# Mixer stage reordered: state-space tiles projected before pool tiles, block copies as transfers, trailing sums on GpSimd

## The chip, the cores and the metric

The kernel runs on one core of a Trainium2 chip. The metric is device time in microseconds (us) from start to end of one execution. The core has five engines that work side by side, each through its own instructions in order: TensorE (PE in the profile, with its weight loads as PEld), VectorE (DVE), ScalarE (ACT), GpSimd (POOL) and SyncE (SP), whose queue here issues nearly all DMAs. They wait for each other on semaphores.

## What is computed

One layer of a decoder for 256 prompt rows and 8 sample rows, model width D = 2048, all weights in float32:

```python
# per layer, c conditions shift, scale and gate (adaLN)
x += 1/2 * g1 * SwiGLU_1(mod1(RMSNorm(x)))              # FFN width 5632
[u ; v] = mod2(RMSNorm(x)) @ W_in                       # u: S5 half, v: pooling half, 1024 each
x += g2 * ([GLU(GELU(Re(C s) + D u)) ; scale * Lin_g(mean_w(v) - v)] @ W_out)
x += 1/2 * g3 * SwiGLU_2(mod3(RMSNorm(x)))
y = RMSNorm(x)
```

s is the state of a diagonal complex recurrence, s_t = A s_(t-1) + B u_t, with 64 groups of 16 channels and 64 states. mean_w is a trailing mean over w = 2, 4, 8, 16 rows, for four groups of 256 channels. The states and the last 15 pooling rows are outputs too.

## The kernel before

**Tiling.** Activations lie with channels on partitions: 16 blocks (kt) of 128 channels by N = 264 columns. A big product is a sum over 16 blocks of k, each in three passes of TensorE (hi·xh, hi·xl, lo·xh, L404 to L406 in `mm3`). The weights come as raw tiles of 512 KB, eight 128x128 blocks each, on SP's queue (L153, five buffers); ScalarE makes the high part hi (L190), VectorE the rest lo (L192). Among them run the "ada" steps: the modulation vectors of later sublayers, eight matmul rows each with two raw tiles of their own (L310), and once in 16 steps a transpose (adaT, L314) and a sum (mod) on VectorE.

**Stages.** FFN1 in groups, the mixer, FFN2, the last norm. The mixer is W_in, the two halves, and W_out. W_in has 16 output tiles. They came in the order 8 to 15 (pooling) and then 0 to 7 (S5). The first FBI = 5 are computed together in `first_block`, k by k, while the normalised input arrives, and the others one by one (48 matmuls each).

**A pool tile** (`pool_tile`): two ScalarE copies out of PSUM, then trailing sums by doubling, w = 16 taking four steps of shifted adds (sA, sB) and w = 2 one; then five small operations make z. All adds ran on VectorE. `pool_lin` multiplies a group's z by its 256x256 matrix pw.

**An S5 tile** ft has four steps. `s5_v`: u is copied out of PSUM (L976), and 16 block copies (L982, half on VectorE and half on ScalarE) lay u out as V, shifted by 64 columns for each of four rows of 32 partitions; two ScalarE operations make bx. `s5_e`: 8 matmuls make E from V and bx (L998), 4 begin y's PSUM tile from V (L1002), 8 add the sample state (L1005). Then a chain of VectorE operations, each on the one before: as, za and zb from E, two scans (L1016), and S in its real and imaginary half. GpSimd meanwhile makes ca from Cm in twelve operations; ca has one buffer. `s5_y`: 32 matmul rows add ca·S to y's PSUM tile (L1050), and GELU follows on ScalarE and VectorE. `s5_g`: one matmul with gluw (L1063), tanh, and the insert into `mixed` on VectorE. `conv` splits `mixed` into Xh and Xl for W_out.

**What sets the order.** The program's text gives the priority, a scheduler of the framework sets one order of instructions for each engine, and the engine then keeps to it: a waiting instruction holds everything behind it. In the text E(ft−1) stands in W_in tile ft after k block 9, y(ft−2) after that tile. The last E, y and g of the S5 tiles stood inside W_out, by `wout_plan`.

Of the kernel before, what the change touches and what calls it, by code (L numbers as in the profile page):

```python
# [50 lines left out]
W_OUT_K = list(range(8, 16)) + list(range(0, 8))  # L51
# [44 lines left out]
def win_order():  # L96
    o = []
    ms = list(range(8, 16)) + list(range(0, 8))
    for kt in range(KT):
        o += [("i", kt, m) for m in ms[:FBI]]  # L100
    for m in ms[FBI:]:
        o += [("i", kt, m) for kt in range(KT)]
    return o


def wout_plan():
    pool, ssm = W_OUT_K[:8], W_OUT_K[8:]
# [9 lines left out]
    mm((2, 3), pool)  # L117
    p += [("g", 6)]
    mm((0, 1, 2, 3), ssm[0:4])
    p += [("y", 7)]  # L120
    mm((0, 1, 2, 3), ssm[4:7])
    p += [("g", 7)]
    mm((4,), pool)
    mm((0, 1, 2, 3), ssm[7:8])
    mm((4,), ssm)
    for m in range(5, KT):
        mm((m,), W_OUT_K)
    return p
# [81 lines left out]
def build(nc, tc, I, O):  # L210
# [459 lines left out]
    def first_block(pool, gh, gl, rb, n):  # L670
# [8 lines left out]
        for i, ps in enumerate(pss):  # L679
            g = pool.tile([P, N], F32, tag=f"fb{i}", name=f"fb{cnt[0]}_{i}", bufs=1)  # L680
# [199 lines left out]
    with tc.tile_pool(name="mix", bufs=1) as mp:  # L880
        mixed = mp.tile([P, KT, N], F32, tag="mixed", name="mixed")
        with tc.tile_pool(name="poolp", bufs=1) as qp:
            rb, samples, one = make_h(qp, mods[3], mods[4], GP)
            pw = qp.tile([P, 4, 2, 256], F32, tag="pw", name="pw")
# [6 lines left out]
            vsm = qp.tile([P, 8, NS], F32, tag="vsm", name="vsm")  # L891

            def pool_tile(mt, ps, z):
# [15 lines left out]
                if w >= 8:  # L909
                    add(sA[:, :, 2:66], sB[:, :, 2:66], sB[:, :, 1:65])  # L910
                    s = sA
                if w >= 16:
                    add(sB[:, :, 2:66], sA[:, :, 2:66], sA[:, :, 0:64])
                    s = sB
# [5 lines left out]
                add(zz[:, SEQ:N], vsm[:, mt, :], hsum[:, mt, :])  # L920
                stt(zz[:, SEQ:N], zz[:, SEQ:N], 1.0 / w, vsm[:, mt, :], ALU.mult, ALU.subtract)

            def pool_lin(g, z):
                for m2 in range(2):
                    ps = bank()
                    for k2 in range(2):
                        T.matmul(ps[:, 0:N], lhsT=pw[:, g, k2, m2 * P:(m2 + 1) * P], rhs=z[:, k2, :], start=(k2 == 0), stop=(k2 == 1))
# [5 lines left out]
            def new_z(g):  # L933
                zs[g] = qp.tile([P, 2, N], F32, tag="z", name=f"z{g}", bufs=3)

            pss = first_block(qp, X1[0], X1[1], rb, FBI)
            for a in range(0, KT, SG):
                for kt in range(a, a + SG):
                    one(kt)
                samples(a, a + SG)  # L940
            tc.keep_in_program_order(nc.sync.dma_start(out=pw, in_=I["poolw"]))

            def u_tile(hook=None):
                ps = bank()
                for kt in range(KT):
                    mm3(ps[:, 0:N], st.get(), Xh[:, kt, 0:N], Xl[:, kt, 0:N], kt == 0, kt == KT - 1)
                    if hook is not None:
                        hook(kt)
                return ps

            for mt in range(FBI):
                if mt % 2 == 0:
                    new_z(mt // 2)
                pool_tile(mt, pss[mt], zs[mt // 2])
            lin = {6: 1, 7: 2, 5: 0}
            for mt in range(FBI, 8):
                ps = u_tile()
                if mt in lin:
                    pool_lin(lin[mt], zs[lin[mt]])
                if mt % 2 == 0:  # L960
                    new_z(mt // 2)
                pool_tile(mt, ps, zs[mt // 2])
            ps = u_tile()
            pool_lin(3, zs[3])
            A.dma_start(out=O["vout"], in_=vout)
            A.dma_start(out=O["vsm"], in_=vsm)

        with tc.tile_pool(name="s5p", bufs=1) as sp:
            Vb = [sp.tile([P, 4, N], F32, tag=f"V{i}", name=f"V{i}") for i in range(2)]
            for t in Vb:  # L970
                GP.memset(t, 0.0)
            S5 = {}

            def s5_v(ft, ps):
# [16 lines left out]
            def s5_e(ft):  # L991
# [17 lines left out]
                a = sp.tile([P, 2, 4, C], F32, tag="za", name=f"za{ft}", bufs=1)  # L1009
                b = sp.tile([P, 4, C], F32, tag="zb", name=f"zb{ft}", bufs=1)  # L1010
# [7 lines left out]
                S = sp.tile([P, 2, 4, C + 1], F32, tag="S", name=f"S{ft}", bufs=2)  # L1018
# [7 lines left out]
                ca = sp.tile([P, 2, 4, 4, 32], F32, tag="ca", name=f"ca{ft}", bufs=1)  # L1026
                cb = sp.tile([P, 4, 2, 32], F32, tag="cb", name=f"cb{ft}", bufs=1)
# [16 lines left out]
            def s5_y(ft):  # L1044
# [6 lines left out]
                y2 = sp.tile([P, N], F32, tag="y2", name=f"y2{ft}", bufs=1)  # L1051
                gy = sp.tile([P, N], F32, tag="gy", name=f"gy{ft}", bufs=1)
# [7 lines left out]
            def s5_g(ft):  # L1060
# [3 lines left out]
                t = sp.tile([P, N], F32, tag="y2", name=f"gt{ft}", bufs=1)  # L1064
# [3 lines left out]
            s5_v(0, ps)  # L1068
# [11 lines left out]
            conved = set()  # L1080

            def conv(kt):
                if kt in conved:
                    return
                conved.add(kt)
                if kt < NFT:
                    A.activation(out=Xh[:, kt, 0:N], in_=mixed[:, kt, :], func=AF.Copy, scale=0.25)
                    stt(Xl[:, kt, 0:N], mixed[:, kt, :], 0.25, Xh[:, kt, 0:N].bitcast(F32), ALU.mult, ALU.subtract)
                else:
                    A.copy(out=Xh[:, kt, 0:N], in_=mixed[:, kt, :])  # L1090
                    sub(Xl[:, kt, 0:N], mixed[:, kt, :], Xh[:, kt, 0:N].bitcast(F32))

# [13 lines left out]
            while plan:  # L1106
# [3 lines left out]
                else:  # L1110
                    {"g": s5_g, "e": s5_e, "y": s5_y}[a[0]](a[1])
                    if a == ("g", 7):
                        break
# [158 lines left out]
```

## Time and profile before

| | us |
|---|---|
| median of three runs (2086.51 to 2089.89) | 2087.66 |
| span of the profiled execution | 2090.6 |
| TensorE busy | 2033.3 (97%) |
| VectorE busy | 1212.7 (58%) |
| ScalarE busy | 842.3 (40%) |
| GpSimd busy | 410.6 (20%) |

No other time of the profiled execution is known than its span. It is within the runs' spread to 0.1%. In the mixer, the first W_in block begins near 954 us from the span's start, the second group at 997, the first E at 1041, the last y ends at 1186, and W_out ends at 1271. To read the rows: a row of the windows view has, for one stretch, each engine's busy time with its count of instructions, then the granted TensorE clock as a share of 2.4 GHz, the busy share of the DMA engines and their rate. A row of the timeline has the start, the duration, the engine, the line, the operation, output<-inputs, the shape and, in brackets, idle time before it and what ended it. Busy time of matmuls is longer at the lower clock, so a stretch can be busy and still lose time.

### The profile page before, as it was taken

The page shows a single profiled execution, that of the slowest core. Times are in us where ns is not written, and L with a number is a line of the kernel's source. Part 1 is how long each engine was busy: PE and PEld are TensorE (multiplying, and loading weights), DVE is VectorE, ACT ScalarE, POOL GpSimd, SP SyncE. Part 2 cuts the span into 40 slices and gives each one's busy share as a digit, 9 for nine tenths or more (in the row PEclk, how much of TensorE's full clock was granted, in tenths as well). Part 3 has the DMA queues.
Part 4 walks back from the last instruction along what each step waited for, and adds up shares of the span by engine and source line. Part 5 has one row for each costly group of instructions (what it writes and reads, how often), then busy time and mean ns, then how long its engine had stood idle before and what let it go on. Part 6 is the DMA issues. An engine that isn't in the chain of part 4 may idle for free.

```text
span 2090.6 us, 41113 instructions
## 1 busy us (share of the span) xinstructions
PE 2033.3 (97%) x16856; PEld 1870.3 (89%) x16856; DVE 1212.7 (58%) x1978; ACT 842.3 (40%) x1258; POOL 410.6 (20%) x713
## 2 busy tenths in 40 slices
PE   6999999999999999999988899999999999999997
PEld 5788999899999989998766698899999999999997
DVE  4665855754444454467789776545555555554555
ACT  4332434433333333355445355433334333334343
POOL 0000100330764068043345332000000000000012
PEclk9999999999999999999989999999999999999998
DMA  8888777777676776777844656875555555555552
GB/s 321 314 296 286 246 261 252 286 267 250 229 247 231 258 252 234 267 261 251 314 151 178 219 205 219 283 273 182 180 175 180 182 187 175 182 182 175 179 181 103
DMA packets 135292, 476.43 MB, mean 228 GB/s; under 512 B 15160, under 2 KB 20152, under 8 KB 134840
## 3 DMA queue, kind: packets, MB, share of 16 engines
q1 hardware_dynamic: 134384, 473.07, 64.6%
q8 instruction: 132, 2.16, 0.4%
q10 hardware_dynamic: 720, 0.75, 0.1%
q14 instruction: 56, 0.46, 0.1%
HBM read 471.20 MB, written 3.01 MB: 227 GB/s over the span
## 4 chain that ended last, share of the span: by engine, by line
PE 71%; issue 11%; POOL 8%; DVE 7%; DMA 2%; ACT 1%; SPq 0%; POOLq 0%; ACTq 0%; DVEq 0%
PE mm L404 22%; PE mm L406 21%; PE mm L405 21%; PE ada_None L310 3%; POOL xu L215 2%; DVE lo L192 2%; PE ada L328 2%; POOL yt L215 1%; DVE V L982 1%; POOL X L215 1%; DMA raw<-ada 1%; POOL acc L215 1%; POOL h L215 1%; DVE S L215 1%; PE E L998 1%
## 5 line engine op out<-in xcount | busy, mean ns | idle before, releaser
L192 DVE TENSOR_TENSOR lo<-raw,hi 128x1024 fp32r<-128x1024 f32 x591 | 733.5, 1241 | 610.4 <-ACT hi L190 584.5
L190 ACT CAST hi<-raw 128x1024 fp32r<-128x1024 f32 x592 | 619.7, 1047 | 1000.6 <-PE mm L405 777.9
L404 PE MATMUL mm<-Xh,hi 128*128 128x264 f32 (+1 forms) x3168 | 922.8, 292 | 2.4 <-ACT Xh L735 1.7
L405 PE MATMUL mm<-Xl,hi 128*128 128x264 f32 (+1 forms) x3168 | 910.6, 288 | 0.0
L406 PE MATMUL mm<-Xh,lo 128*128 128x264 f32 (+1 forms) x3168 | 906.6, 287 | 1.7 <-DVE lo L192 1.5
L404 PEld LDWEIGHTS mm<-Xh,hi 128*128 128x128 f32 x3168 | 600.6, 190 | 77.3 <-issue 59.8
L406 PEld LDWEIGHTS mm<-Xh,lo 128*128 128x128 f32 x3168 | 602.8, 191 | 8.8 <-issue 5.6
L405 PEld LDWEIGHTS mm<-Xl,hi 128*128 128x128 f32 x3168 | 602.5, 190 | 7.9 <-issue 7.6
L404 PE MATMUL mm<-ah,hi 128*128 128x264 f32 x1408 | 404.3, 287 | 0.0
L406 PE MATMUL mm<-ah,lo 128*128 128x264 f32 x1408 | 400.7, 285 | 0.0
L405 PE MATMUL mm<-al,hi 128*128 128x264 f32 x1408 | 398.8, 283 | 0.0
L404 PEld LDWEIGHTS mm<-ah,hi 128*128 128x128 f32 x1408 | 264.9, 188 | 21.0 <-issue 15.9
L405 PEld LDWEIGHTS mm<-al,hi 128*128 128x128 f32 x1408 | 265.3, 188 | 0.0
L406 PEld LDWEIGHTS mm<-ah,lo 128*128 128x128 f32 x1408 | 264.7, 188 | 0.0
L215 POOL TENSOR_TENSOR acc<-acc,sq 128x264 f32<-128x264 f32 x42 | 45.8, 1089 | 748.5 <-ACT sq L655 748.5
L310 PE MATMUL ada_None<-raw,sc 128*32 128x512 f32 x896 | 129.0, 608 | 8.2 <-DVE adaT_None L314 5.0
L232 DVE SCALAR_TENSOR_TENSOR x<-mm,mod,x 128x256 f32<-128x256 f32 x78 | 37.6, 482 | 42.1 <-PE mm L406 42.1
L215 DVE TENSOR_TENSOR s<-s,mm 128x264 f32<-128x264 f32 x68 | 29.1, 428 | 55.7 <-PE mm L406 55.7
L328 PE MATMUL ada<-raw,sc 128*32 128x256 f32 (+1 forms) x640 | 43.8, 374 | 14.0 <-DMA raw<-ada 13.9
L215 POOL TENSOR_TENSOR xu<-X,apow 128x128 f32<-128x128 f32 x96 | 53.6, 579 | 3.8
L215 POOL TENSOR_TENSOR s<-s,partBuT 128x264 f32<-128x264 f32 x7 | 5.3, 755 | 219.4 <-DVE partBuT L215 203.0
L310 PEld LDWEIGHTS ada_None<-raw,sc 128*32 128x32 f32 x896 | 19.3, 108 | 29.8 <-DMA raw<-ada 9.3
(303 smaller groups left out, 1471.6 us busy)
## 6 DMA issues: line engine op xcount, KB each, us to landing
raw<-w SPq DMA_DIRECT2D x528, 512.0 KB, 3.8
raw<-ada SPq DMA_DIRECT2D x288, 512.0 KB, 5.2
raw<-win SPq DMA_DIRECT2D x32, 512.0 KB, 5.1
raw<-wout SPq DMA_DIRECT2D x32, 512.0 KB, 4.3
x<-x SPq DMA_DIRECT2D x4, 528.0 KB, 5.7
xin<-x SPq DMA_DIRECT2D x16, 132.0 KB, 3.7
y<-o SPq DMA_DIRECT2D x7, 264.0 KB, 2.7
Cm<-Cm SPq DMA_DIRECT2D x1, 1024.0 KB, 5.8
```

Source lines behind the costliest of these rows:

```text
L190: c = self.nc.scalar.copy(out=hi, in_=raw)
L192: e.tensor_tensor(out=lo, in0=raw, in1=hi.bitcast(F32), op=ALU.subtract)
L215: return e.tensor_tensor(out=out, in0=a, in1=b, op=op)
L232: return e.scalar_tensor_tensor(out=out, in0=a, scalar=s, in1=b, op0=op0, op1=op1)
L310: T.matmul(ps[32 * j:32 * j + 32, :], lhsT=sc[:, kt, :], rhs=raws[j // 2][:, (j % 2) * 512:(j % 2 + 1) * 512], start=(kt == 0), stop=(kt = ...
L328: mm = T.matmul(o, lhsT=sc[:, kt, :], rhs=r[:, t, :, j, :], start=(kt == 0), stop=(kt == KT - 1))
L404: T.matmul(ps, lhsT=hi, rhs=xh, start=start, stop=False)
L405: T.matmul(ps, lhsT=hi, rhs=xl, start=False, stop=False)
L406: T.matmul(ps, lhsT=lo, rhs=xh, start=False, stop=stop)
L982: e(out=v[32 * tau:32 * tau + 32, q, 64 * tau:64 * tau + n], in_=u[32 * q:32 * q + 32, 0:n])
L998: T.matmul(E[:, ri, q * 72:(q + 1) * 72], lhsT=bx[:, ri, q].rearrange("p a b -> p (a b)"), rhs=v[:, q, 192:N], start=True, stop=True)
```

## The change

W_in's tiles come in the order 0 to 7 (S5), then 14, 15, 12, 13, 10, 11, 8, 9 (pool, widest window first). u goes straight into the places of `mixed` that pool tiles take later, and the 16 block copies of a tile are 16 DMAs from SBUF to SBUF on SP's queue, of 8 to 33 KB. The shifted adds and the sample sum run on GpSimd. In the text E(i) stands after k block 9 of the i-th single tile and y(i−1) behind that tile, so that all E, y and g lie inside W_in and none inside W_out; `pool_lin` of the groups 3, 2, 1 lie among the pool tiles, that of group 0 in W_out after 14 k blocks. pw comes in four loads rather than one. z has two buffers, not three. One pool ("heads") holds what two held in turn. FFN1 and the rest of the program keep their order.

```diff
-W_OUT_K = list(range(8, 16)) + list(range(0, 8))
+V_M = [14, 15, 12, 13, 10, 11, 8, 9]
+W_IN_M = list(range(8)) + V_M
+W_OUT_K = list(range(8)) + V_M
...
 def wout_plan():
...
-    mm((0, 1), pool[0:4])
-    p += [("g", 5), ("e", 7)]
-    mm((0, 1), pool[4:8])
-    p += [("y", 6)]
...
+    mm((0, 1), W_OUT_K[:14])
+    p.append(("l", 0))
+    mm((0, 1), W_OUT_K[14:])
+    for m in range(2, KT):
         mm((m,), W_OUT_K)
...
                 def sh2(o, s, d):
-                    add(o[:, d:4, 2:66], s[:, d:4, 2:66], s[:, 0:4 - d, 2:66])
-                    add(o[:, 0:d, 2:66], s[:, 0:d, 2:66], s[:, 4 - d:4, 1:65])
+                    add(o[:, d:4, 2:66], s[:, d:4, 2:66], s[:, 0:4 - d, 2:66], GP)
+                    add(o[:, 0:d, 2:66], s[:, 0:d, 2:66], s[:, 4 - d:4, 1:65], GP)
...
-                zs[g] = qp.tile([P, 2, N], F32, tag="z", name=f"z{g}", bufs=3)
...
+                pw = qp.tile([P, 2, 256], F32, tag="pw", name=f"pw{g}", bufs=2)
+                tc.keep_in_program_order(nc.sync.dma_start(out=pw, in_=I["poolw"][:, g]))
+                zs[g] = qp.tile([P, 2, N], F32, tag="z", name=f"z{g}", bufs=2), pw
...
-                u = sp.tile([P, N], F32, tag="u", name=f"u{ft}", bufs=1)
-                A.copy(out=u, in_=ps[:, 0:N])
+            def s5_v(ft):
+                u = mixed[:, V_M[ft], :]
                 v = Vb[ft % 2]
                 for q in range(4):
                     for tau in range(4):
                         n = N if tau == 0 else SEQ - 64 * tau
-                        e = (V.tensor_copy, A.copy)[(q + tau) % 2]
-                        e(out=v[32 * tau:32 * tau + 32, q, 64 * tau:64 * tau + n], in_=u[32 * q:32 * q + 32, 0:n])
...
+                        nc.sync.dma_start(out=v[32 * tau:32 * tau + 32, q, 64 * tau:64 * tau + n], in_=u[32 * q:32 * q + 32, 0:n])
...
-            for ft in range(1, NFT):
-                def hook(kt):
-                    if kt == 14 and ft >= 3:
-                        s5_g(ft - 3)
-                    if kt == 9:
-                        s5_e(ft - 1)
-                ps = u_tile(hook)
-                s5_v(ft, ps)
-                if ft >= 2:
-                    s5_y(ft - 2)
...
+            s5_v(0)
+            lin = {5: 3, 7: 2, 9: 1}
+            for i in range(KT - FBI):
+                ps = bank()
+                for kt in range(KT):
+                    mm3(ps[:, 0:N], st.get(), Xh[:, kt, 0:N], Xl[:, kt, 0:N], kt == 0, kt == KT - 1)
+                    if kt == 9 and i < NFT:
+                        s5_e(i)
+                    if kt == 14 and 2 <= i < NFT + 2:
+                        s5_g(i - 2)
...
+                if i + 1 < NFT:
+                    s5_v(i + 1)
+                if 1 <= i < NFT + 1:
+                    s5_y(i - 1)
+                if i in lin:
+                    pool_lin(lin[i])
```

**TensorE, E to y, before.** The third S5 tile's E, and y of the second behind it (a number in a name tells tiles apart; E_12475 is the third E, S_12307 comes from the second, E_12274).

```order
L998 MATMUL E_12475<-V_12038,bx_12366 128x72 x8
L1002 MATMUL mm_12484<-V_12038,KTp 32x264 x4
L1005 MATMUL mm_12484<-as_93,Cm 32x8 x8
L404 MATMUL mm_12411<-Xh,hi_12262 128x264
...
L1063 MATMUL mm_12546<-gy_12405,gluw 128x264
...
L1050 MATMUL mm_12283<-S_12307,ca_12316 32x64 x32
L310 MATMUL ada_None<-raw_12422,sc 32x512 x2
```

Left out are 14 W_in matmuls ahead of the gluw row and three behind it; y uses the S of the E before the one above.

**TensorE, E to y, after.** The third S5 tile from the middle of its E rows to the fourth tile's first E.

```order
L975 MATMUL E_12027<-V_11094,bx_11923 128x72 x5
L979 MATMUL mm_12036<-V_11094,KTp 32x264
L982 MATMUL mm_12036<-as_93,Cm 32x8 x8
L394 MATMUL mm_12168<-Xh,hi_12015 128x264
...
L300 MATMUL ada_None<-raw_11981,sc 32x512 x2
...
L1027 MATMUL mm_12036<-S_12060,ca_12069 32x64 x32
L300 MATMUL ada_None<-raw_12019,sc 32x512 x2
L975 MATMUL E_12219<-V_11095,bx_12123 128x72
```

S_12060 is made from E_12027, the E above it: between the Cm row and y stand 24 W_in matmuls and one ada step, and the next E stands one ada row behind y.

**VectorE, the chain in an S5 tile, before.** The second half of the second tile's chain (the row of L1016 is a scan).

```order
L215 TENSOR_TENSOR S_12307<-za_12297,Wr 128x4x64
L1016 SCALAR_TENSOR_TENSOR za_12297<-dec_12220,za_12297 128x256
L982 COPY V_12038<-u_12348 32x264
L215 TENSOR_TENSOR zb_12298<-za_12297,Wi 128x256
L215 TENSOR_TENSOR S_12307<-za_12297,Wr 128x4x64
L215 TENSOR_TENSOR S_12307<-S_12307,zb_12298 128x4x64
L982 COPY V_12038<-u_12348 32x128
L215 TENSOR_TENSOR zb_12298<-za_12297,Wi 128x256
```

**VectorE, the same place after**, in the fourth tile (z_12300 belongs to pool group 3, sB is a sum from GpSimd, sm a constant).

```order
L205 TENSOR_TENSOR S_12252<-S_12252,zb_12243 128x4x64
L222 SCALAR_TENSOR_TENSOR z_12300<-sB,vp_11085 128x256
L205 TENSOR_TENSOR zb_12243<-za_12242,Wi 128x256
L205 TENSOR_TENSOR z_12300<-sB,sm 128x4x4
L222 SCALAR_TENSOR_TENSOR z_12300<-z_12300,vsm 128x8
L205 TENSOR_TENSOR S_12252<-S_12252,zb_12243 128x4x64
```

The V copies are gone from the chain; in this tile z operations that need GpSimd's sB stand inside it.

On SP's queue, where raw tiles alone stood, the 16 transfers of a tile now stand in a row, with about five raw tiles between one tile's and the next; the four pw parts stand among them.

## Rows read from the trace of the kernel before

**Rows 1.** Page, part 1: busy time, share of the span, instructions of each engine.

```profile
PE 2033.3 (97%) x16856; PEld 1870.3 (89%) x16856; DVE 1212.7 (58%) x1978; ACT 842.3 (40%) x1258; POOL 410.6 (20%) x713
```

**Rows 2.** Windows: stretch, length, busy PE, PEld, DVE, ACT, POOL, clock, DMA share, GB/s.

```profile
953.00:1040.00 87.00, 85.46 (x609) 67.36 (x608) 67.74 (x176) 43.11 (x92) 26.85 (x49) 1.00 0.80 290
1050.00:1170.00 120.00, 100.69 (x1155) 82.49 (x1155) 110.88 (x208) 55.65 (x125) 63.71 (x103) 0.83 0.42 151
1170.00:1210.00 40.00, 37.34 (x330) 28.43 (x330) 25.61 (x44) 17.05 (x31) 11.55 (x18) 1.00 0.78 283
```

**Rows 3.** Waits of PE, 1050 to 1170: waiter <- releaser: us, times, longest.

```profile
PE E L998 <- DVE V L982: 10.6, 12, 1.6
PE ada_None L310 <- DVE adaT_None L314: 5.0, 1, 5.0
PE E L998 <- ACT gy L1053: 3.1, 2, 2.3
```

**Rows 4.** Windows of 10 us in the S5 stretch, columns as in rows 2.

```profile
1060.00:1070.00 10.00, 5.01 (x41) 3.34 (x33) 9.48 (x17) 5.02 (x13) 9.53 (x15) 0.90 0.30 107
1070.00:1080.00 10.00, 10.00 (x71) 8.26 (x64) 5.46 (x13) 1.33 (x2) 0.00 (x0) 0.58 0.60 211
...
1130.00:1140.00 10.00, 8.94 (x129) 6.86 (x127) 9.32 (x15) 6.28 (x17) 8.67 (x16) 1.00 0.30 107
```

**Rows 5.** Timeline of PE: start, us, line, operation, [idle before <-releaser].

```profile
1002.00 0.28 PE L405 MATMUL mm<-Xl,hi 128*128 128x264 f32 x1
...
1002.99 0.28 PE L404 MATMUL mm<-Xh,hi 128*128 128x264 f32 x1
...
1046.26 1.07 PE L310 MATMUL ada_None<-raw,sc 128*32 128x512 f32 x8
...
1058.93 1.10 PE L1050 MATMUL mm<-S,ca 128*32 128x64 f32 x64
...
1069.17 1.93 PE L310 MATMUL ada_None<-raw,sc 128*32 128x512 f32 x8 [4.99 <-DVE adaT_None L314]
...
1105.85 1.31 PE L998 MATMUL E<-V,bx 128*128 128x72 f32 x10 [1.08 <-DVE V L982]
...
1122.08 2.38 PE L998 MATMUL E<-V,bx 128*128 128x72 f32 x10 [0.81 <-DVE V L982]
```

**Rows 6.** Timeline of DVE, one S5 chain from as to its last S.

```profile
1109.70 0.21 DVE L215 TENSOR_TENSOR as<-as,E 128x64 f32<-128x64 f32 x1
...
1113.46 0.41 DVE L232 SCALAR_TENSOR_TENSOR mixed<-gt,gy 128x264 f32<-128x264 f32 x1
...
1115.85 0.82 DVE L982 COPY V<-u 32x264 f32<-32x264 f32 x1
...
1117.04 0.53 DVE L982 COPY V<-u 32x128 f32<-32x128 f32 x1
1117.60 0.75 DVE L215 TENSOR_TENSOR S<-S,zb 128x256 f32<-128x256 f32 x1
```

**Rows 7.** Groups of DVE, 1050 to 1170: xcount | busy us, mean ns | idle before.

```profile
L982 DVE COPY V<-u 32x128 f32<-32x128 f32 (+3 forms) x55 | 30.7, 558 | 2.0 <-ACT u L976 0.8
L192 DVE TENSOR_TENSOR lo<-raw,hi 128x1024 fp32r<-128x1024 f32 x14 | 19.3, 1385 | 0.1
...
L314 DVE STREAM_TRANSPOSE adaT_None<-ada_None 128x512 f32<-128x512 f32 x1 | 0.7, 701 | 0.0
```

**Rows 8.** Tile S, whole span: xcount, ns min/median/max, first to last start, forms.

```profile
L215 DVE TENSOR_TENSOR S<-S,zb x16: 404/750/954, 1049.7 to 1174.2; 128x256 f32<-128x256 f32 x16
```

**Rows 9.** Tile ca, whole span, columns as in rows 8.

```profile
L215 POOL TENSOR_TENSOR ca<-Cm,apow x32: 612/717/1678, 1037.9 to 1170.8; 128x256 f32<-128x256 f32 x32
```

**Rows 10.** Tile win's raw loads, columns as in rows 8, and their landing time.

```profile
L153 SPq DMA_DIRECT2D raw<-win x32: 327/371/976, 937.2 to 1109.3; - x32
...
DMA to landing us min/median/max: 3.4/5.1/7.5
```

**Rows 11.** DMA issues: tiles, queue, count, KB each, median us to landing.

```profile
y<-o SPq DMA_DIRECT2D x2, 132.0 KB, 1.8
```

More of the change, by code (lines that the diff above doesn't have):

```diff
@@ L97, in win_order @@
     o = []
-    ms = list(range(8, 16)) + list(range(0, 8))
     for kt in range(KT):
-        o += [("i", kt, m) for m in ms[:FBI]]
-    for m in ms[FBI:]:
+        o += [("i", kt, m) for m in W_IN_M[:FBI]]
+    for m in W_IN_M[FBI:]:
         o += [("i", kt, m) for kt in range(KT)]
@@ L679, in first_block @@
         for i, ps in enumerate(pss):
-            g = pool.tile([P, N], F32, tag=f"fb{i}", name=f"fb{cnt[0]}_{i}", bufs=1)
+            g = dst[i] if dst else pool.tile([P, N], F32, tag=f"fb{i}", name=f"fb{cnt[0]}_{i}", bufs=1)
             s8 = pool.tile([P, NM], F32, tag=f"fs{i}", name=f"fs{cnt[0]}_{i}", bufs=1)
@@ L881, in build, with conv, wo_mm @@
         mixed = mp.tile([P, KT, N], F32, tag="mixed", name="mixed")
-        with tc.tile_pool(name="poolp", bufs=1) as qp:
+        pss = {}
+        plan = wout_plan()
+        conved = set()
+        def conv(kt):
+            if kt in conved:
+                return
+            conved.add(kt)
+            if kt < NFT:
+                A.activation(out=Xh[:, kt, 0:N], in_=mixed[:, kt, :], func=AF.Copy, scale=0.25)
+                stt(Xl[:, kt, 0:N], mixed[:, kt, :], 0.25, Xh[:, kt, 0:N].bitcast(F32), ALU.mult, ALU.subtract)
+            else:
+                A.copy(out=Xh[:, kt, 0:N], in_=mixed[:, kt, :])
+                sub(Xl[:, kt, 0:N], mixed[:, kt, :], Xh[:, kt, 0:N].bitcast(F32))
+        def wo_mm(kt, m):
+            conv(kt)
+            if m not in pss:
+                pss[m] = bank()
+            mm3(pss[m][:, 0:N], st.get(), Xh[:, kt, 0:N], Xl[:, kt, 0:N], kt == W_OUT_K[0], kt == W_OUT_K[-1])
+        with tc.tile_pool(name="heads", bufs=1) as qp:
             rb, samples, one = make_h(qp, mods[3], mods[4], GP)
-            pw = qp.tile([P, 4, 2, 256], F32, tag="pw", name="pw")
             vps = [qp.tile([P, 4, 66], F32, tag=f"vp{i}", name=f"vp{i}") for i in range(2)]
@@ L891, in build @@
             vsm = qp.tile([P, 8, NS], F32, tag="vsm", name="vsm")
+            Vb = [qp.tile([P, 4, N], F32, tag=f"V{i}", name=f"V{i}") for i in range(2)]
+            for t in Vb:
+                GP.memset(t, 0.0)
+            S5 = {}
             def pool_tile(mt, ps, z):
@@ L926, in pool_lin @@
                     for k2 in range(2):
[L927 removed]
+                        T.matmul(ps[:, 0:N], lhsT=pw[:, k2, m2 * P:(m2 + 1) * P], rhs=z[:, k2, :], start=(k2 == 0), stop=(k2 == 1))
                     mt = 2 * g + m2
@@ L1093, in build @@
-            plan = wout_plan()
-            pss = {}
-            def wo_mm(kt, m):
-                conv(kt)
-                if m not in pss:
-                    if m == 2:
-                        pe2 = pse.tile([P, 2, 512], F32, tag="E", name="pe2", bufs=1)
-                        pss[2], pss[3] = pe2[:, 0], pe2[:, 1]
-                    else:
-                        pss[m] = bank()
-                mm3(pss[m][:, 0:N], st.get(), Xh[:, kt, 0:N], Xl[:, kt, 0:N], kt == W_OUT_K[0], kt == W_OUT_K[-1])
+            fb = [mixed[:, V_M[ft], :] for ft in range(FBI)]
@@ new lines, in build @@
+            first_block(qp, X1[0], X1[1], rb, FBI, fb)
+            for a in range(0, KT, SG):
+                for kt in range(a, a + SG):
+                    one(kt)
+                samples(a, a + SG)
+            s5_v(0)
[8 more added lines that the diff above has]
+                        s5_g(i - 2)
+                    if i == KT - FBI - 1 and 2 <= kt < 10:
+                        conv(kt - 2)
+                ft = FBI + i
+                if ft < NFT:
+                    A.copy(out=mixed[:, V_M[ft], :], in_=ps[:, 0:N])
+                else:
+                    mt = V_M[ft - NFT] - 8
+                    if mt // 2 not in zs:
+                        new_z(mt // 2)
+                    pool_tile(mt, ps, zs[mt // 2][0])
+                if i + 1 < NFT:
[4 more added lines that the diff above has]
+                    pool_lin(lin[i])
@@ L1115, in build @@
-            A.dma_start(out=O["ss"], in_=as0)
+                if a[0] == "l":
+                    pool_lin(a[1])
+                    break
+                wo_mm(a[1], a[2])
         with tc.tile_pool(name="tail", bufs=1) as wq:
```

101 lines of the change are left out of this document (21 added, 80 removed).

## Prediction

> **What bounds the kernel now.** I read the page's part 1 first: TensorE is busy for 2033.3 of 2090.6 us [rows 1], so anything outside the mixer can only be won by giving TensorE less work, and the change takes no matmul away. Then I cut the mixer into stretches. In the first W_in block and the pool tiles TensorE is busy 85.46 of 87 us at full clock, with VectorE at 67.74: the pool sums that VectorE does there are hidden. In the state-space (S5) stretch, 1050 to 1170, TensorE is busy 100.69 of 120 us and its mean granted clock is 0.83, while VectorE is busy 110.88 us. In 1170 to 1210 only 2.7 us are idle [rows 2]. So all that this kernel can lose or win in the mixer lies in one stretch: 120 − 100.69 = 19.3 us idle, and (1 − 0.83) × 100.69 = 17.1 us that busy work lost to the lower clock. Together 36.4 us.
>
> The waits say what the idle time is: E stands waiting for V's block copies on VectorE 12 times, 10.6 us, and once 5.0 us for the adaT transpose [rows 3], both queued on the full VectorE. The clock follows idle time. In 1060 to 1070 TensorE was busy 5.01 of 10 us; in the next 10 us it was busy throughout, at a mean granted clock of 0.58, that is mostly 1.2 GHz. In 1130 to 1140 it lost only 1.06 us, and the clock stayed at 1.00 [rows 4]. Ten E matmuls take 1.31 us at 2.4 GHz and 2.38 us at 1.2 [rows 5]. The timeline has five such slow stretches, each behind a wait, of which [rows 5] show two; they make the 17.1 us, so 3.4 us each.
>
> The time between the chain's ends is hidden before: y (the product of S and ca) of one tile stands behind E of the **next**, so the VectorE chain from E to S has a whole W_in tile as cover, and y on S is not among the large waits of [rows 3].
>
> **The change part by part.**
> *V by transfers.* Removes 64 VectorE and 64 ScalarE copies. On VectorE that is 55 × 0.558 = 30.7 us of the 110.88 in the stretch [rows 7], about 4.5 us a tile, and it takes the E waits (10.6 us) with it. In the place of the copies come 16 transfers a tile on SP's queue, the one that feeds the weights. E(n) now stands about a tile after u(n), so a landing of 3.4 to 7.5 us (w_in's raws) or 1.8 us (the 132 KB stores) [rows 10, 11] is covered for every tile but the first, where I put 1 us.
>
> *The order on TensorE.* This decides. In the new order E(n) has slipped by about a tile, and y(n) has not: both stand in one W_in tile, and the next E follows y(n) at once. TensorE has to wait out the chain E → as, za, zb, scans, S → y with only the matmuls between as cover. One W_in matmul costs (1002.99 − 1002.00)/8 = 0.124 us, one ada step of eight rows 1.0 us (1.07 with its tail), the y rows 0.95 us [rows 5]. Counting the rows between the last E/Cm row and y(n):
> y0, y2, y4, y6: 24 W_in matmuls and one ada step, 3.95 us each; y1: 6 and 1.5 steps, 2.25; y3: 9 and 1.5, 2.6; y5: 24 and 1.5, 4.45; y7: 34 and 1.5, 5.7. Sum 30.8 us.
> The chain: from as to the last S VectorE needed 1109.70 to 1118.35 = 8.65 us, of which 0.41 + 0.82 + 0.53 were an insert and two V copies, so 6.9 [rows 6]. To this come 0.3 us from TensorE to as, and one lo, since one stands inside or ahead of each chain in the new order: 19.3/14 = 1.38 [rows 7], of which I take 1.3. Off go 0.5: half of the y rows need S's real half only. c = 8.0 us; eight tiles 64 us.
> Extras: at y3 four z operations of the pool tiles are inserted (0.8, as two of 0.41 in [rows 6]), and one waits on the GpSimd sums that stand behind ca (1.5, half of a tile's sums, below); at y5 the adaT transpose, 0.70 [rows 7], and mod behind it, for which I take 0.6; at y7 two more inserts, 0.8. Sum 4.4.
> Idle time after: 64 − 30.8 + 4.4 = **37.6 us**, in place of 19.3. It replaces it rather than adds to it: the V waits are gone, and the adaT transpose is counted among the extras.
>
> *Clock.* Seven of these waits are 4 to 8 us long, one about 3. Each is followed by E at once. The rows of before say that a 5 us loss in 10 is followed by 1.2 GHz [rows 4, 5]. Seven at 3.0 us (a little under the 3.4 of before, since part of a slow stretch will end inside the next wait) are **21 us** in place of 17.1.
>
> *Pool sums to GpSimd.* VectorE loses work that was hidden [rows 2]; in the S5 tiles it would have cost it 2 to 3 us a tile, so the sums' move is right once the pool tiles lie there. GpSimd gets, for w = 16, four adds of 256 elements. One add took 0.717 us there [rows 9], so 2.9, with its copies about 3.5 us a tile, beside twelve such operations for ca, 8.7, and about 0.8 for dec: 13.0 us. ca's one buffer is free only after y(n), and must be full before y(n+1), some 19 us later in my sum (11.6 of work, 4.7 idle, 2.6 clock), so it is hidden; a slowing of GpSimd by 40% would end that.
> While GpSimd works, VectorE's S←S,zb takes 750 ns at the median and 404 at best [rows 8]. If eight such operations of a chain were each slowed by 0.35, c is 10 rather than 8, 16 us in all: my upper bound. If the lo falls ahead of the chain's start in part, c is 7.5, the lower.
> The Trainium skill, SBUF — State Buffer, section Who interferes with whom, says that a VectorE instruction with two SBUF inputs and a GpSimd instruction that reads SBUF shut each other out of a shared port. The row of S←S,zb agrees. By the rule every added GpSimd sum that falls into a chain would cost the chain about its own length, at most 2.9 us, which is about the upper bound above.
>
> *Small things.* E's 16 rows are cut into about four groups; a change of kind of row costs between nothing and 0.28 − 0.124 = 0.16 us [rows 5]: 24 such, 0 to 3.8, I take 2.4. pw in four parts, memsets ahead of h, and the dma scratch are at nothing: 1.5 us of idle time in 87 [rows 2] show that none of it stands on the path. W_out starts with the S5 tiles, all done by then, and its last pool product stands after 14 of 16 k's: I leave the 2.7 idle us of 1170 to 1210 as they are.
>
> **Sum:** 37.6 − 19.3 + 21 − 17.1 + 2.4 + 1.0 = +25.6 on the profiled 2090.6 us. The three runs have a median of 2087.7, 0.14% below the profiled one, so 2113 us. Ends: c = 7.5 (33.6 idle), clock 10, small 2: +9, 2097. c = 10 (53.6), eight slow stretches at 3.4 (27), small 3.4: +48, 2135.
>
> **The rivals.**
> *The chain is covered.* VectorE without its copies is the relief that the change is made of. If the order's cover were enough, all 36.4 us would be won, less 3.4: 2055 us. It needs E to y in 3.9 us; the chain's own operations took 6.9 [rows 6]. I give it 0.10, mostly for a reading of the order that is wrong.
> *The clock holds.* The waits come evenly, one a tile, rather than in bursts. If TensorE stays at 2.4 GHz through them, as after the 1.06 us of 1130 to 1140 [rows 4], then c = 7.5 gives 33.6 − 19.3 − 17.1 + 2 = −1, 2087 us: no change. The 4.99 us wait ahead of the row at 1069.17 [rows 5] speaks against. 0.13, of which 0.03 below 2083.
> *SP's queue is the bound (slower).* Eight completion semaphores go round on SP, so each of the 21 transfers of a tile waits for the one eight before it, and weights queue behind V rows. 21/8 landings a tile: 13.4 us at the 5.1 of the w_in raws, 19.7 at 7.5 [rows 10]. It decides where the landing is above 7.2 us, against 18.9 us of my tile. At 8 us a tile takes 21.0, 15 us more over seven tiles: 2128. The transfers' 8 to 33 KB speak against: one of 132 KB landed in 1.8 us [rows 11]. 0.07.
> The Trainium skill, DMA: Bandwidth & Descriptors, section Rules for kernel authors, says to merge many small transfers, since under 64 KB one pays mostly overhead. All 128 lie under it. By that rule the landing would not fall with the size, and this rival is nearer than the row of 1.8 us makes it; no run shown here has such a transfer.
>
> **How the numbers follow.** My forecast holds 0.70, 2097 to 2135. 0.2% (4.2 us) is about what a measurement of this kernel tells from none. Faster: 0.10 + 0.03 = 0.13. Same: 0.10, of the held clock. Slower: 0.70 + 0.07 = 0.77. The range 2084 to 2140 leaves out the covered chain, the little below 2083, and the far part of SP's rival.
>
> **What would show it.** In the changed kernel's trace the y rows wait on VectorE's S eight times for 30 to 40 us in all; E's waits on V are near nothing; E follows E at 17 to 19 us; the mean clock over the S5 tiles is at or below 0.83; VectorE's busy share there falls from 0.92 to about 0.75. I am wrong if y's waits are under 2 us each, if the clock there is above 0.95, or if ScalarE's hi waits for raws.

## The result and the profile after

The changed kernel takes 2130.12 us (median of five runs, 2127.71 to 2130.24) against 2089.89 us in the same runs: a ratio of 1.0179, interval 1.0161 to 1.0198, **40 us slower**. The forecast was 2113 in a range of 2084 to 2140. Sign and range held. The size did not quite (+25 forecast), and below it turns out that the sum came near largely by luck.

The profiled execution has a span of 2125.9 us, 35.3 more than before. The page's first part, as [rows 1]:

```profile
PE 2066.7 (97%) x16856; PEld 1873.2 (88%) x16856; DVE 1168.9 (55%) x1872; ACT 820.4 (39%) x1189; POOL 431.2 (20%) x755
```

TensorE ran the same 16856 instructions and was **busy** 33.4 us longer; its idle time grew by 1.9 us only. The windows, with the columns of [rows 2], say where: the first W_in block, the S5 tiles, and what follows them to the end of W_out.

```profile
953.00:1000.00 47.00, 40.78 (x285) 32.86 (x285) 36.16 (x69) 23.62 (x44) 27.67 (x45) 0.93 0.66 233
...
1005.00:1165.00 160.00, 141.89 (x1319) 98.65 (x1318) 91.17 (x186) 41.95 (x78) 88.98 (x148) 0.91 0.47 163
1169.00:1311.00 142.00, 140.38 (x991) 114.83 (x990) 81.47 (x136) 65.33 (x126) 25.24 (x54) 1.00 0.68 235
```

VectorE is relieved: 91.17 of 160 us, where it was 110.88 of 120 [rows 2]. The S5 tiles' idle time is 160 − 141.89 = 18.1 us, about the 19.3 of before, and the clock there is 0.91, better than 0.83. Yet the stretch is longer. TensorE's waits over the mixer (950 to 1300), as in [rows 3]:

```profile
PE mm L1027 <- DVE S L205: 8.9, 5, 2.2
PE mm L394 <- ACT hi L180: 6.8, 4, 1.7
PE mm L701 <- DVE dg L218: 6.0, 1, 6.0
PE ada_None L300 <- DMA raw<-ada: 2.3, 2, 1.2
PE mm L396 <- DVE lo L182: 1.8, 3, 1.5
```

E no longer waits for V. In its place y (L1027) waits on S, five times in three of the eight tiles, the first W_in block waits 6.0 us for dg (the matrix with the norm's factor, made on VectorE), and W_in matmuls wait for hi in four tiles, 1.7 us each time. The loss is in rows that count as busy. TensorE's timeline (columns of [rows 5]) in two S5 tiles:

```profile
1038.09 0.41 PE L979 MATMUL mm<-V,KTp 128*32 128x264 f32 x1
...
1038.34 0.39 PE L979 MATMUL mm<-V,KTp 128*32 128x264 f32 x1
...
1039.68 1.41 PE L300 MATMUL ada_None<-raw,sc 128*32 128x512 f32 x8
...
1045.22 1.94 PE L1027 MATMUL mm<-S,ca 128*32 128x64 f32 x64 [2.01 <-DVE S L205]
...
1163.63 1.05 PE L300 MATMUL ada_None<-raw,sc 128*32 128x512 f32 x4
1165.42 1.05 PE L300 MATMUL ada_None<-raw,sc 128*32 128x512 f32 x4
```

An ada step of eight rows took 1.07 us [rows 5]; a **half step of four rows takes 1.05**. Its rows write four different parts of 32 partitions and run side by side (four of them start within 0.02 us of each other): cut in two, each half takes as long as the whole. The same is true of the four KTp products of a tile, about 0.65 us for the eight rows together before, and now 0.39 to 0.63 us for one or two.

To see all of it I sum, for equal work (from the first W_in block's start, at 952 us, to one and the same row of FFN2, at 1319 before and 1355 after), the time from each row's start to the next row's start by the kind of row, idle time apart. This is worked out from the timelines, in us:

| | before | after | change |
|---|---|---|---|
| ada | 46.4 | 66.5 | +20.2 |
| KTp | 5.8 | 16.8 | +11.0 |
| E | 23.4 | 17.7 | −5.7 |
| W_in and W_out matmuls | 244.5 | 248.3 | +3.9 |
| y, Cm, glu, pool product and the rest | 23.0 | 26.7 | +3.7 |
| idle | 24.1 | 26.5 | +2.4 |
| whole stretch | 367.2 | 402.7 | +35.5 |

The first two lines are 31 of the 35.5 us. Rows count at the clock that they ran at. By the trace's record of the granted clock, the rows lost 18.0 us to the lower clock before and 15.4 after, of which ada 0.9 and 3.9: the clock makes 3 us of ada's line and is no large part of the whole.

What cut them? The order in the program's text keeps them together. The scheduler places rows by its own picture of when data comes; with 16 transfers a tile on SP's queue it sees V's four column blocks arrive one by one, and the two raw tiles of an ada step apart. What the scheduler sees is an inference. That the transfers bring the cuts is shown by the runs below, in both orders of tiles: with copies in their place KTp and nearly all ada steps stand whole, and the kernel before with transfers has both cut. SP's timeline (DMAs issued, us of SP's time):

```profile
1002.81 0.33 SPq L143 DMA_DIRECT2D raw<-ada  x1
1003.74 10.46 SPq L959 DMA_DIRECT2D V<-mixed  x16
1014.31 0.53 SPq L143 DMA_DIRECT2D raw<-win  x1
```

The 16 transfers of a tile occupy SP for 10.46 us, and no weight is issued in that time.

### The profile page after: what moved, and what is told of

The parts are those of the page before. It is cut to its first block, busy times and chain, and to the rows that moved or that the text cites. A ratio compares the mean times of both kernels' runs of the same rounds, so it can differ in the third digit from the quotient of the medians.

```text
span 2125.9 us, 41169 instructions
## 1 busy us (share of the span) xinstructions
PE 2066.7 (97%) x16856; PEld 1873.2 (88%) x16856; DVE 1168.9 (55%) x1872; ACT 820.4 (39%) x1189; POOL 431.2 (20%) x755
## 4 chain that ended last, share of the span: by engine, by line
PE 84%; issue 6%; DVE 3%; POOL 3%; DMA 2%; ACT 1%; SPq 1%; POOLq 0%; ACTq 0%; DVEq 0%
PE mm L394 25%; PE mm L396 24%; PE mm L395 24%; PE ada_None L300 5%; PE ada L318 2%; DVE lo L182 1%; POOL acc L205 1%; PE mm L979 1%; DMA raw<-w 1%; DMA raw<-ada 1%; PE E L975 1%; DMA raw<-win 0%; SPq L959 0%; POOL xu L205 0%; ACT hi L180 0%
## 5 line engine op out<-in xcount | busy, mean ns | idle before, releaser
L394 PE MATMUL mm<-Xh,hi 128*128 128x264 f32 (+1 forms) x3200 | 932.4, 292 | 8.6 <-ACT hi L180 7.0
L396 PE MATMUL mm<-Xh,lo 128*128 128x264 f32 (+1 forms) x3200 | 916.8, 287 | 3.4 <-DVE lo L182 3.1
L394 PEld LDWEIGHTS mm<-ah,hi 128*128 128x128 f32 x1408 | 264.9, 188 | 21.0 <-issue 15.9
L300 PE MATMUL ada_None<-raw,sc 128*32 128x512 f32 x896 | 150.1, 614 | 3.0 <-DMA raw<-ada 2.9
L205 POOL TENSOR_TENSOR X<-xu,xu 128x128 f32<-128x128 f32 x64 | 44.7, 699 | 5.0
```

The source lines that it names most:

```text
L205: return e.tensor_tensor(out=out, in0=a, in1=b, op=op)
L300: T.matmul(ps[32 * j:32 * j + 32, :], lhsT=sc[:, kt, :], rhs=raws[j // 2][:, (j % 2) * 512:(j % 2 + 1) * 512], start=(kt == 0), stop=(kt = ...
L394: T.matmul(ps, lhsT=hi, rhs=xh, start=start, stop=False)
L396: T.matmul(ps, lhsT=lo, rhs=xh, start=False, stop=stop)
```

## The experiments

All on the chip, each beside the kernel before in the same runs. Its median there was 2090.40, 2091.78, 2093.05 or 2093.75 us, so a gain in us against the 2130.12 of the changed kernel can be off by some 3 us; the ratio is to the kernel before. "Ada", "KTp" and "idle" are the table's lines, summed in the same way over each run.

**Ada steps whole.** The changed kernel; rows pinned behind each other in the mixer only.

```diff
-        for j in range(4):
-            T.matmul(ps[32 * j:32 * j + 32, :], lhsT=sc[:, kt, :], rhs=raws[j // 2][:, (j % 2) * 512:(j % 2 + 1) * 512],
+        for n, j in enumerate((2, 3, 0, 1)):
+            mm = T.matmul(ps[32 * j:32 * j + 32, :], lhsT=sc[:, kt, :], rhs=raws[j // 2][:, (j % 2) * 512:(j % 2 + 1) * 512],
...
+            if n and whole:
+                tc.keep_in_program_order(mm)
```

> The changed kernel, with the eight matmul rows of an ada step kept in one run on TensorE in the mixer (there they stood as 41 half steps of about 1.05 us, as long as a whole one of 1.07). Theory of cut runs: rows that write different 32-column parts run side by side, so a half costs as much as a whole; 20 steps win 1.0 us each: 2130 - 20 = 2110. Rival, the chain: halves between the Cm rows and y only fill time in which TensorE would wait for S, so only those outside the S5 tiles count: about -10, 2120, and the waits of y on S grow by as much as the halves shrink. Rival, SP's queue: the halves fill waits for late raw tiles: 2130.

2116.55 us, 1.0119 (1.0102 to 1.0136): 14 us won, between the two theories. Ada falls by 24.3 us to 42.3, and idle time rises by 11.8 to 38.3: half of what the halves cost came back as waits. They are not the rival's, since y's waits on S hardly grew (8.9 to 9.4 us over the mixer). Matmuls of W_in and W_out now wait for lo (7.2 us there, 1.8 in the changed kernel), ada for its raw tiles (5.5 and 2.3) and y once for GpSimd (2.9). In the S5 tiles (1005 to 1160):

```profile
PE mm L1031 <- DVE S L205: 8.5, 5, 6.4
PE mm L397 <- ACT hi L180: 5.8, 4, 1.7
PE mm L399 <- DVE lo L182: 4.2, 4, 1.1
PE ada_None L301 <- DMA raw<-ada: 4.0, 3, 2.5
```

**KTp whole.** One line, and the scheduler's order follows: 48 W_in matmuls of cover for every y.

```diff
-                    T.matmul(yp[32 * q:32 * q + 32, 0:N], lhsT=KTp[:, q0 + q, :], rhs=v[:, q, :], start=True, stop=False)
+                    tc.keep_in_program_order(T.matmul(yp[32 * q:32 * q + 32, 0:N], lhsT=KTp[:, q0 + q, :], rhs=v[:, q, :], start=True, stop=False))
```

> The changed kernel, with the four KTp products of a tile kept in a row behind E. The scheduler's order changes with it: 48 W_in matmuls between the Cm rows and y rather than 6 to 34, and 19 ada half steps rather than 41. Cut runs: KTp wins 11 us (16.8 to 5.8 in the ledger of the two traces) and 22 halves 11 us: 2108. Chain: the cover ends the waits of y on S, 13 us more with their clock: 2090 to 2097. SP's queue as the bound: the waits move to hi for raws, 2120 to 2130.

2103.81 us, 1.0059 (1.0043 to 1.0076): 26 us won, a little more than the 22 expected of the cut runs alone. KTp falls by 12.2 us; ada only by 4.0, so the 11 us for fewer halves were wrong. Another 7.8 us went from the W_in and W_out matmuls: 3.2 of it is the clock, and most of the rest comes of fewer changes of kind of row. By the timelines each change costs the matmuls beside it 0.18 us, and there are 57 here, as in the kernel before, where the changed kernel has 88. The waits of y on S fall from 8.9 to 5.8, but E's rows, most of which now stand together, wait on the transfers:

```profile
PE E L975 <- DMA V<-mixed: 9.9, 5, 2.1
...
PE mm L1027 <- DVE S L205: 5.8, 5, 2.3
```

**Both.**

> Both of these: ada steps whole, KTp in a row, 48 W_in matmuls of cover for each y. Cut runs and chain together: 2130 - 20 - 11 - 13 = 2086, the level of the kernel before or a little under. Cut runs alone: 2099. SP's queue as the bound: 2115 to 2130, with hi waiting for raws in each tile.

2106.13 us, 1.0071 (1.0056 to 1.0086): in none of the three ranges; the two do not add. Ada and KTp are back at 42.4 and 5.4 us, below the kernel before, and 36.6 us of idle time stand in their place: E waits 11.2 us for V's transfers and y 13.3 for S. The lower clock takes 22.8 us from the rows, where it took 15.4 in the changed kernel. The chain of waits from 1005 to 1145 (shares of that window by line) now leads through SP's issues, which are a quarter of it:

```profile
by line: SPq L963 27.1%; PE E L979 7.6%; DMA V<-mixed 6.1%; PE ada_None L301 5.5%; PE mm L397 5.4%; PE mm L399 4.9%; PE mm L398 4.8%; DMA raw<-ada 4.0%; PE mm L946 3.5%; issue 3.4%; DVE lo L182 3.1%; PE mm L983 2.9%; POOL ca L205 2.8%; DMA 
```

So behind the cut runs SP's queue is the next bound, at 0.59 us (median in the changed kernel) for one issue.

**The first tile's ca held behind h** (GpSimd's rows pinned behind the last h row; TensorE's order is unchanged).

```diff
+                return nullcontext() if ft else tc.issue_after(mark[0])
...
+                    with held(ft):
+                        mul(c0, cr, pr, GP)
```

> The changed kernel, with the first tile's dec and ca held on GpSimd behind the normalised input h. TensorE's order is the same. Theory: these GpSimd operations shut VectorE's tiny rstd operations out (0.55 us rather than 0.17 each), which gave the one wait of 6.0 us for dg in the first W_in block; without them the wait is under 1 us and the clock dip behind it goes: 2121 to 2124. Rival: the wait comes from the lo split standing among them on VectorE, or h's own delay replaces it: 2128 to 2130.

2130.72 us, 1.0190 (1.0175 to 1.0205): nothing won. That is the rival's time, though the wait did come from these operations: it fell from 6.0 us to 1.7, and the first block ended 4.0 us earlier, at 998.66 rather than 1002.69. Then the first E waited for V's transfers and started at 1008.59, where it had started at 1008.60:

```profile
PE E L980 <- DMA V<-mixed: 3.5, 1, 3.5
PE mm L394 <- ACT hi L180: 1.7, 1, 1.7
PE mm L701 <- DVE dg L218: 1.7, 1, 1.7
```

SP began the first tile's transfers at 1003.74 in the changed kernel and at 1004.79 here. What held them is this run's own edit: ca, held behind h, stood in GpSimd's queue ahead of the small sum that completes u in `mixed`, and SP waited for that sum, 5.5 us where it had been 0.5 (SP's waits, 999 to 1012):

```profile
SPq L963 <- POOL mixed L205: 5.5, 1, 5.5
```

So this run moves GpSimd's work from one wait to another, and what the 6.0 us are worth by themselves is not shown. The profile's later 5 us of difference stay unexplained.

**Halves in the kernel before**, 57 of them, one block of three matmuls between the halves.

```diff
+        half((0, 1))
+        if cut:
+            return half, last
...
+        if st.rest:
+            i, (half, last) = st.rest.pop(0)
+            half((2, 3))
```

> The kernel before, with the ada steps of the mixer cut into two halves, one W_in or W_out block of three matmuls between: 57 half runs in place of 30 whole ones; nothing else in TensorE's order differs. It prices the cut by itself. Theory: a half costs as much as a whole, 28 x 1.0 us, less what the S5 tiles' waits for V take up (about 11 of them): 2090 + 17 to 28 = 2107 to 2118. Rival: the halves cost nothing of their own (in the changed kernel they were a sign of late raw tiles): 2090.

2104.68 us, 1.0059 (1.0038 to 1.0080): +13 us, somewhat under the range. Ada rose by 24.3 us, to 70.7: the price of a cut step, 0.9 us, holds in a kernel without any transfers. Idle time fell from 24.1 to 12.0, so half of the cost lay where TensorE waited anyway. That is the mirror of the first run: **a cut costs its full price only where nothing else is late.**

**Copies back**, half on VectorE and half on ScalarE, the rest as changed.

```diff
-                        nc.sync.dma_start(out=v[32 * tau:32 * tau + 32, q, 64 * tau:64 * tau + n], in_=u[32 * q:32 * q + 32, 0:n])
+                        e = (V.tensor_copy, A.copy)[(q + tau) % 2]
+                        e(out=v[32 * tau:32 * tau + 32, q, 64 * tau:64 * tau + n], in_=u[32 * q:32 * q + 32, 0:n])
```

> The changed kernel with V's block copies on VectorE and ScalarE again, half each; tile order, pool sums on GpSimd and all else as changed. The scheduler then keeps the ada steps and KTp whole and puts y behind the next tile's E (66 matmuls of cover). Theory, the transfers carry the loss: 2130 - 32 (cut runs) - 13 (waits of y) + some 10 (VectorE full again, E waits for V) = 2088 to 2098. Rival, the loss lies in projecting S5 first or in the sums: above 2110.

2100.42 us, 1.0044 (1.0028 to 1.0060), just above the range: 30 of the 40 us are gone with the transfers. Ada and KTp are 49.6 and 3.8 us. New waits, 19.8 us of glu for gy and 7.6 for an adaT transpose, take the place of what was won beyond that.

**Transfers alone in the kernel before** is the counterpart (the same diff, the other way round).

> The kernel before with one part of the change alone: V's 16 block copies a tile as transfers on SP's queue. TensorE's order changes by itself as in the changed kernel: KTp in 32 single rows, 19 ada halves, 6 to 24 W_in matmuls between the Cm rows and y (96 for the last). Theory, this part carries the loss: KTp +11, halves +9, waits of y and hi some 10, less about half of the 13.9 us of E's waits and their clock: 2105 to 2118. Rival, the transfers cost only where S5 tiles come first, and here relieve VectorE: 2075 to 2090.

2107.52 us, 1.0062 (1.0042 to 1.0082), +14 us. The order cuts KTp (15.9 us) and 19 ada halves (58.8 us), as forecast, and y waits on S for 8.8 us. Here E's 13.9 us of waits and VectorE's load go, which pays for part.

**All copies on ScalarE.**

> The same with all 16 copies of a tile on ScalarE (16 x 0.324 = 5.2 us a tile beside its 7 or so). VectorE keeps its relief of 4.5 us a tile, SP issues raw tiles only, TensorE's order as in the run before. If the relief of VectorE was worth what the kernel before lost in the S5 tiles, 36 us in part: 2065 to 2080. Rival: ScalarE's hi comes late behind its copies: 2090 to 2100, with waits on hi. Rival: the E to S chain or the clock holds it: 2085 to 2090.

2097.02 us, 1.0025 (1.0013 to 1.0037): still 5 us slower than the kernel before, and far from the 2065 to 2080 that the theory gave. The time is that of the rival with hi, but not the reason: TensorE waits for hi nowhere. The chain has a new member: VectorE, in the middle of making S, waits for GpSimd's sum, and TensorE's glu waits 17.3 us for gy behind it. VectorE's timeline:

```profile
1066.87 0.82 DVE L222 SCALAR_TENSOR_TENSOR z<-sB,vp 128x256 f32<-128x256 f32 x1 [4.78 <-POOL sB L205]
1067.62 0.94 DVE L205 TENSOR_TENSOR S<-S,zb 128x256 f32<-128x256 f32 x1
...
1085.43 0.82 DVE L222 SCALAR_TENSOR_TENSOR z<-sB,vp 128x256 f32<-128x256 f32 x1 [5.74 <-POOL sB L205]
```

**Sums back on VectorE**, in the changed kernel (TensorE's order unchanged).

```diff
-                    add(o[:, d:4, 2:66], s[:, d:4, 2:66], s[:, 0:4 - d, 2:66], GP)
+                    add(o[:, d:4, 2:66], s[:, d:4, 2:66], s[:, 0:4 - d, 2:66])
```

> The changed kernel with the trailing sums on VectorE again; TensorE's order is the same. Theory: the move of the sums decides nothing: 2127 to 2133. Rival, GpSimd's sums shut VectorE's chain out: 8 to 16 us less, 2114 to 2122, with shorter times from as to S. Rival, the sums in VectorE's queue lengthen the chains: 5 to 10 us more.

2122.64 us, 1.0147 (1.0129 to 1.0164): 7.5 us won by the times, 9 by the ratios, so the theory that the move decides nothing was wrong. y's waits on S fall from 8.9 to 4.8 us (one more of 1.7 is put down to sA, now on VectorE), and VectorE's waits on GpSimd's sums (5.0 us for sB, 10.8 in all, in the changed kernel's S5 tiles) are gone. That is the dependence on sums behind ca, not a general slowing of the chain: in the five tiles without pool work or adaT inside, as to the last S takes 7.1 us in both kernels, and in the other three it falls from 9.3 to 9.6 us to 7.3 to 8.7.

**Copies on ScalarE and sums on VectorE**: of the three parts in the title only the reorder is left (the kernel before had half of the copies on VectorE).

> The run with copies on ScalarE, with the trailing sums on VectorE again as well: of the change only the reorder is left. In that run VectorE sat 4.8 and 5.7 us in the S5 chain for sB from GpSimd, and TensorE 17.3 us for gy behind it. Theory, GpSimd was the bound there (ca 8.7 and sums 3.5 us a tile, slowed): those waits go, 2097 - 17 = 2080, better than the kernel before. Rival: VectorE takes the sums (2 to 3 us a tile in four tiles) and the same waits return under its own name: 2090 to 2097.

2095.03 us, 1.0011 (1.0001 to 1.0020): the rival was right, and the reorder in this form neither wins nor loses. The waits for sB went, and the same glu waits came back under VectorE's name, since its operations take twice their time while GpSimd makes ca:

```profile
PE mm L1040 <- DVE gy L222: 14.0, 5, 4.2
PE ada_None L300 <- DVE adaT_None L304: 7.4, 1, 7.4
```
```profile
1064.15 0.84 DVE L205 TENSOR_TENSOR sB<-sA 128x256 f32<-128x256 f32 x1
1064.91 0.95 DVE L222 SCALAR_TENSOR_TENSOR gy<-y,gy 128x264 f32<-128x264 f32 x1
1065.78 0.84 DVE L222 SCALAR_TENSOR_TENSOR z<-sB,vp 128x256 f32<-128x256 f32 x1
```

**Transfers on ScalarE's queue**, sums on GpSimd.

> The changed kernel with V's 16 transfers a tile issued by ScalarE's queue, not SP's; sums on GpSimd. Theory, SP's queue: 16 issues took 10 to 12 us a tile on SP, in which no weight was issued; off it the waits of TensorE for hi (6.8 us) and the scheduler's cut runs (ada halves 3 in place of 41 in the order) go: 2095 to 2105. Rival: the issues hold up ScalarE's hi in their place, 10 us a tile beside 7: 2115 to 2130.

2118.57 us, 1.0126 (1.0108 to 1.0143). The rival's time, not quite its reason: ada falls to 50.6 and the waits for hi go, but one issue takes ScalarE's queue 0.60 us, as long as SP's, KTp and E wait 19.8 us, most of it for V, and glu 8.7 for gy. KTp stays cut (15.0 us). The transfers' issue time is the trouble on either queue.

**Everything together**: copies on ScalarE, sums on VectorE, ada and KTp whole, the first ca held, y and g half a tile later in the text.

```diff
-                    if kt == 14 and 2 <= i < NFT + 2:
-                        s5_g(i - 2)
+                    if kt == 1 and 3 <= i < NFT + 3:
+                        s5_g(i - 3)
+                    if kt == 5 and 2 <= i < NFT + 2:
+                        s5_y(i - 2)
```

> That run and, besides, ada steps and KTp kept whole, the first tile's ca held behind h, and y and g each moved later by about half a W_in tile in the text (84 W_in matmuls between the Cm rows and y). Sum from the waits of the runs before: dg 6.0 to 1.7 (-4), halves left 2, y and g with more cover: 2070 to 2078. Rival, as when ca was held alone: the first block's gain is given back by E waiting for V: 2080. Rival: ca's one buffer makes GpSimd late for y: 2085.

2083.35 us, 0.9958 (0.9945 to 0.9970): faster than both kernels, by 0.4% against the one before, though not in the forecast range. The wait for dg and half of glu's are gone; idle time is still 28.0 us, most of it waits of ada for raw tiles (8.6), of glu (7.3), of the first E (3.9) and of a pool product for z (3.6). Which of its parts the gain over the run before comes from is not shown.

## Why the prediction was right, point by point

The direction and the range came out, but by the prediction's own signs its main mechanism mostly did not, and that the sum came near is luck in good part: most of the idle time that it added up was not there, and the cost that was there it had put at 2.4 us.

**Which stretch.** Right: all of the difference arose in the mixer (35.5 us in the table, 35.3 in the spans).

**The order on TensorE: E and y in one W_in tile.** The mechanism is there in part: y waits on S in the place of E on V, but in three tiles of eight. Its size was wrong. I had 37.6 us of idle time; the S5 tiles have 18.1, and 8.9 of it stand ahead of y. (That more cover shortens these waits is not shown: with 48 matmuls ahead of every y they were 5.8 us in one run and 13.3 in the other.) The chain itself was well read: from the end of the Cm rows to the last S 7.2 us in the tiles without extras, against c = 8.0, ends 7.5 and 10. The cover was not. Ahead of y0 I counted 3.95 us; 8.73 stood there: 24 matmuls, two half steps of 1.73 and 1.43 us at the lower clock, a wait of 1.69 for hi. The failed step is the **price of one ada step at 1.0 us, taken from a whole step, for pieces which the order already showed as halves** (its rows name one raw tile each, with matmuls between). Over the eight tiles 57 us stood between the Cm rows and y rather than the 30.8 counted: some 10 more by halves, 9.2 of other waits (6.9 for hi, 2.3 for ada's raw tiles), and the rest by the lower clock and changes of kind of row. Most of it took the place of waits of y. One sum is off too: eight operations slowed by 0.35 us add 2.8, so that upper bound is c = 10.8 and not 10.

**"E's 16 rows cut into about four groups", 0 to 3.8 us.** This is the term that was the loss, and it was mis-sized by the same step: I priced a change of kind of row, which was about right (0.18 us each, 31 more of them), and not four products that lose their neighbours. At 2.4 us in the sum it measured +11.0 us for KTp and +20.2 for the halves. That the total came out near was luck: a rise of idle time of 18.3 us that was only 2.4 stood against 31 us that it lacked.

**Clock.** 21 us forecast in place of 17.1. The S5 tiles' mean was 0.91, so (1 − 0.91) × 141.9 = 12.8, and the first block lost 2.9. By the trace's clock record TensorE ran at 1.2 GHz five times in the S5 tiles, as before, but for 27 us together and not 41; "at or below 0.83" was wrong.

**V by transfers.** Landing was as cheap as the 132 KB store suggested, 1.8 us at 8 KB and 2.4 at 33 KB, and E waited for V in no tile. What I did not cost was issue time: 0.59 us each. My rival on SP's queue was priced by landings; priced by issues it is 16 × 0.59 = 9.4 us a tile, still under the tile's 20.0 us. With ada and KTp both whole, E waits 11.2 us for V, and SP's issues are the largest part of the chain of waits.

The Trainium skill, DMA: Bandwidth & Descriptors, section Rules for kernel authors, says of many small transfers to make one large one, as under 64 KB one pays mostly overhead. The landing times agree: four times the bytes cost 0.6 us more.

**Small things at nothing.** Wrong for the first tile's dec and ca ahead of h. While GpSimd ran them, VectorE's little rstd operations took three times as long. Before, in 962 to 963:

```profile
962.39 0.17 DVE L232 SCALAR_TENSOR_TENSOR rs<-rs 128x3 f32<-128x3 f32 x1
962.59 0.17 DVE L215 TENSOR_TENSOR rs<-rs 128x3 f32<-128x3 f32 x1
```

and after:

```profile
963.39 0.23 DVE L219 TENSOR_SCALAR rs<-rs 128x3 int32<-128x3 int32 x1
963.66 0.53 DVE L222 SCALAR_TENSOR_TENSOR rs<-rs 128x3 f32<-128x3 f32 x1
964.22 0.58 DVE L205 TENSOR_TENSOR rs<-rs 128x3 f32<-128x3 f32 x1
```

A cover of 1.5 idle us in 87 said that the path was full, not that it had room. In place of nothing stand 6.0 us of waiting and 2.9 of clock in the first block; the run that held ca back gave them back at the first transfers, so what they are worth by themselves stays open.

The Trainium skill, SBUF — State Buffer, section Who interferes with whom, has a VectorE instruction with two SBUF inputs contend with a GpSimd instruction that reads SBUF, over a shared pair of ports that it calls an exclusive lock. These rows agree: operations with two inputs go from 0.17 to 0.53 and 0.58 us, near the 0.61 of one GpSimd operation, and the one with a single input only to 0.23. I had applied the rule to long operations; here it weighed most on short ones, three times as long where those of 128 x 256 took twice as long.

**Sums on GpSimd.** "Right once the pool tiles lie there" was wrong: with them back on VectorE the changed kernel is 7.5 us faster. I had 1.5 us for one z operation that waits for sums behind ca; VectorE's waits on GpSimd's sums came to 10.8 us in the S5 tiles.

**The signs I named.** y's waits on S, mostly no: not eight times for 30 to 40 us but five times, 1.8 us at the mean, 8.9 in all, and under 2 us each was the first sign of being wrong; E's waits near nothing, yes; E to E 20.0 us ((1148.75 − 1008.60)/7), a little over 17 to 19; clock 0.91, no; VectorE's share 0.57, lower than 0.75. "Wrong if ScalarE's hi waits for raws": no, TensorE's 6.8 us for hi come of bx. bx has one buffer, waits for E's end, and the next hi stands behind it on ScalarE (TensorE resumes at 1019.98):

```profile
1017.65 1.33 ACT L962 ACTIVATE bx<-BuT,sm 128x512 f32<-128x512 f32 x2 [4.58 <-PE E L975]
1018.90 1.03 ACT L180 CAST hi<-raw 128x1024 fp32r<-128x1024 f32 x1
```

These four waits stand in the four tiles in which y then waited for nothing behind 24 matmuls and two halves: part of the wait that I had put ahead of y stood there, a few rows earlier.

## What to carry to other kernels

Rows that run side by side on TensorE (products into different parts of 32 partitions) have one price for the group: when an order shows such a group cut, multiply, and look whether the pieces stand where TensorE waits anyway. When a scheduler decides the order, ask what a new transfer makes it believe about arrival times; here one line that pins four products gave back 26 of 40 us. Price small DMAs by the time that they hold the issuing queue, and check what is queued behind. When a run moves work off one wait, look at what the work now stands in front of, before calling the wait worthless.

## What the hardware showed that I had not expected

An ada step of eight rows takes 1.07 us and its half 1.05. One DMA issue held SP 0.59 us and ScalarE's queue 0.60 (median of 128), where the landing took 1.8. Operations of VectorE on 128 x 3 elements took 0.53 to 0.58 us rather than 0.17 beside GpSimd's elementwise work, and those on 128 x 256 took 0.84 to 0.95 rather than 0.41.

The Trainium skill, TensorEngine Tiling (Array Packing), section Key Properties, says that tiles of the array operate independently, and different ones can run in parallel. The 1.05 and 1.07 us of half and whole steps agree.
